# Two squared-ReLU FFNs: from up and down in turn to all up first, then down as seven Strassen products

## The chip, the core and the metric

The kernel runs on one core of a Trainium2 chip. It has a matmul engine (TensorE, PE in the profile, with its weight loads as PEld), three engines for elementwise work (VectorE, DVE; ScalarE, ACT; GpSimd, POOL), a sync engine (SP) that issues all DMAs of this kernel in its own order, and 16 DMA engines. The metric is the time of one execution on the device in microseconds, as the median of several runs.

## The reference

Two transformer blocks, one after the other, on 1024 tokens of width 1024, all in float32. The first mixes tokens by a gated delta rule and by latent attention, the second by a short convolution and stick-breaking attention. Each ends with the FFN that this change is about:

```python
D_MODEL, SEQ, D_FF = 1024, 1024, 4096
# block 1
h = rms_norm(x, ffn_pre_norm[l])
f = jnp.square(jax.nn.relu(h @ w_up[l])) @ w_down[l]
x = x + rms_norm(f, ffn_post_norm[l])
# block 2
h2 = modulate(rms_norm_2(x, g_pre_mlp[l]), sh2, sc2)      # mod = c @ w_ada[l] + b_ada[l]
ff = jnp.square(jax.nn.relu(h2 @ w_mlp_in[l])) @ w_mlp_out[l]
x = x + gt2[:, None, :] * rms_norm_2(ff, g_post_mlp[l])
```

## The kernel before, in words

Every float32 product is made of three matmuls: each operand is split into a part `hi` in a rounded 32-bit format and a rest `lo`, and `mm3` (L166 to L171) adds hi hi, hi lo and lo hi in PSUM. `load_w` (L182) loads 1 MB of weights into one buffer (`w_raw`, a single one), casts it on ACT to `w_hi` (L200, in two halves) and subtracts on DVE to `w_lo` (L206); of `w_hi` and `w_lo` there are two each. `split` (L173) does the same for other tiles.

The two FFNs run in `ffn` (L962). The 4096 columns of `w_up` are cut into 16 chunks of 256; the 1024 tokens into two halves of 512. `up(c, half)` makes two tiles of 128 features x 512 tokens, 24 matmuls each, in feature order, so that a tile is the stationary operand of the down projection as it stands. ACT applies ReLU and the square (L975, L976), DVE squares again and subtracts for the `lo` part (L977, L978). `down(c, half)` multiplies chunk c by 256 rows of `w_down`: for each of 4 token tiles and 2 halves of the 1024 output columns 6 matmuls in PSUM, and DVE adds the result to `y` in SBUF (L1019; `y` holds all 1024 tokens). So up and down alternate, and nothing of f leaves SBUF. In the first FFN `side(c)` works off the modulation of block 2 beside it: `modulation_acc` (L1050) loads four pieces of `w_ada`, one buffer `ada_raw`, and adds their rows on DVE; `modulation_sum` has a matmul, and `modulation_columns` makes `amod` and `mod` out of them.

An `epilogue` (L925) finishes a tile of 128 tokens: it squares `y` on ACT, multiplies by the gain (`yg`, POOL or DVE), takes the inverse root on DVE (`rsqrt`, L212, small operations), adds the residual (`xt`) and stores it. `norm_to_hT` (L267) then normalizes, transposes on PE (L281) and splits into `h_hi` and `h_lo`, the next layer's input. The out projection ahead of each FFN does the first four token tiles, then the last four, so the second half of h comes later than the first; the order of the first steps in `ffn` (L1023 to L1030) is made for that.

A scheduler puts the instructions of each engine in a fixed order, by priority (the order in the program, `tc.high_priority` ahead of it) and by its own estimate of times. A tile's buffers are handed out in turn; a new tile waits until the old one's users are done. Each engine, SP too, then works strictly in its order.

Of the kernel before, what the change touches and what calls it, by code (L numbers as in the profile page):

```python
# [8 lines left out]
F32 = mybir.dt.float32  # L9
# [16 lines left out]
# columns of the constant array  # L26
# [11 lines left out]
}  # L38
FSLOTS = 3

# rows of the vector table (columns once transposed)
# [4 lines left out]
def constants():  # L46
# [6 lines left out]
    # from the first to the second 32 of each 64  # L53
# [11 lines left out]
def tile_two_blocks(ctx: ExitStack, tc: tile.TileContext, I, out):  # L65
# [9 lines left out]
    class Ring:  # L75
        # a pool for each buffer: a new pool waits for all that its memory was used for, so the smaller the sooner
# [40 lines left out]
    def interleave(*streams, bg=None):  # L117
        # streams of (generator, total cost): emit so that all of them advance evenly;
        # bg: one more that is left where it stands when the others have ended
# [14 lines left out]
    # ------------------------------------------------------------------ scratch in DRAM  # L134
# [21 lines left out]
    mix_dr = scratch("mix", (D, S))  # L156

    # ------------------------------------------------------------------ helpers
# [53 lines left out]
    def rsqrt(ssq, scale, eps, n=1, name="rs", pool=None):  # L212
        # v^-1/2, v = scale ssq + eps: a first guess from the bits of v (within 3.5%), three Newton steps
# [27 lines left out]
    # ------------------------------------------------------------------ constants  # L241
# [11 lines left out]
    def columns(st):  # L253
# [50 lines left out]
    # ------------------------------------------------------------------ block 1: projections  # L304
# [7 lines left out]
    def rotary(p1, cs, fr, posi):  # L312
# [20 lines left out]
        # token-major: cos cos -sin sin  # L333
# [6 lines left out]
    def rotary_T(p1, cs, csC, csS):  # L340
        # feature-major, four heads: (cos cos) x 4 and (-sin sin) x 4
# [10 lines left out]
    def block1_low_rank(h, px, p1, wkp, cqT, ckT, cs):  # L352
# [26 lines left out]
            # both halves of k by themselves; the second one comes where the next weights lie later  # L379
# [67 lines left out]
            # decay and write strength: la = -exp(a_log) softplus(ga + dt_bias), beta = sigmoid(gb)  # L447
# [17 lines left out]
    def mla_up(pa, cqT, ckT, csC, csS):  # L465
# [28 lines left out]
        # columns regrouped: nope of all heads, rope of all heads, rope with its halves swapped  # L494
# [32 lines left out]
    # silu(gate) * out_norm  # L527
# [16 lines left out]
    # q, k, v: causal convolution, silu  # L544
# [32 lines left out]
    # ------------------------------------------------------------------ block 1: gated delta rule  # L577
    # chunks of 128 tokens, four heads side by side
# [26 lines left out]
    def blocks_of(t, c, b):  # L605
        # block b of chunk c in each head: [row, head, column]
# [4 lines left out]
    # all that needs neither q nor v: normalized k, decays, A = strictly lower part of beta k k^T decay  # L611
    def gdn_keys(kp):
# [3 lines left out]
        # exp of: cumulative decay, decay to the chunk's end, whole chunk's decay  # L616
# [6 lines left out]
        def head(hd, k):  # L623
            # four chunks of a head side by side
# [778 lines left out]
```

## Time and profile before

| | us |
|---|---|
| median of 3 runs | 2857.09 (2855.22 to 2857.35) |
| span of the profiled execution, first to last instruction | 2851.6 |
| PE busy in that span | 2787.7 |
| first FFN, first up matmul to the last down matmul, about | 653.7 to 1385 |
| second FFN, the same, about | 2138 to 2838 |

The profile is of one execution. It gives for each engine the busy time and the time of every instruction; a wait is put down to what released it. Matmuls are pipelined: the length shown of one is not the step from one to the next.

### The profile page before, as it was taken

The page shows a single profiled execution, that of the slowest core. Times are in us where ns is not written, and L with a number is a line of the kernel's source. Part 1 is how long each engine was busy: PE and PEld are TensorE (multiplying, and loading weights), DVE is VectorE, ACT ScalarE, POOL GpSimd, SP SyncE. Part 2 cuts the span into 40 slices and gives each one's busy share as a digit, 9 for nine tenths or more (in the row PEclk, how much of TensorE's full clock was granted, in tenths as well). Part 3 has the DMA queues.
Part 4 walks back from the last instruction along what each step waited for, and adds up shares of the span by engine and source line. Part 5 has one row for each costly group of instructions (what it writes and reads, how often), then busy time and mean ns, then how long its engine had stood idle before and what let it go on. Part 6 is the DMA issues. An engine that isn't in the chain of part 4 may idle for free. (4 is left out here: it accounts for less than half of the span.)

```text
span 2851.6 us, 39066 instructions
## 1 busy us (share of the span) xinstructions
PE 2787.7 (98%) x14568; PEld 2362.7 (83%) x14568; DVE 1837.8 (64%) x3805; ACT 1079.8 (38%) x2083; POOL 363.6 (13%) x472
## 2 busy tenths in 40 slices
PE   7999999999999999999999999999999999999998
PEld 7788889898787787878898888887898888888886
DVE  7668699868677666557833258776477454444457
ACT  5544666555311212124621146563266221121122
POOL 1242353211000000001200022112212000000000
PEclk9999999999999999999999999999999999999999
DMA  4386486355433233113441545445754211111124
GB/s 129 93 289 197 153 236 166 123 166 184 146 96 111 89 96 94 55 60 128 168 152 63 173 135 154 128 128 164 249 178 155 74 59 45 45 60 36 54 85 144
DMA packets 306885, 360.84 MB, mean 127 GB/s; under 512 B 29844, under 2 KB 240891, under 8 KB 306695
## 3 DMA queue, kind: packets, MB, share of 16 engines
q1 hardware_dynamic: 306694, 358.35, 39.6%
q8 instruction: 115, 1.88, 0.3%
q14 instruction: 76, 0.61, 0.1%
HBM read 278.80 MB, written 79.48 MB: 126 GB/s over the span
## 5 line engine op out<-in xcount | busy, mean ns | idle before, releaser
L170 PE MATMUL mm<-h_hi,w_hi 128*128 128x512 f32 x1760 | 690.5, 392 | 0.0
L170 PE MATMUL mm<-h_lo,w_hi 128*128 128x512 f32 x1760 | 689.1, 392 | 0.0
L170 PE MATMUL mm<-h_hi,w_lo 128*128 128x512 f32 x1760 | 688.1, 391 | 0.0
L170 PE MATMUL mm<-w_hi,f 128*128 128x512 f32 x2048 | 649.0, 393 | 1.8 <-ACT w_hi L200 1.1
L200 ACT CAST w_hi<-w_raw 128x1024 fp32r<-128x1024 f32 (+1 forms) x282 | 282.3, 1047 | 616.4 <-PE mm L170 470.0
L206 DVE TENSOR_TENSOR w_lo<-w_raw,w_hi 128x1024 fp32r<-128x1024 f32 (+1 forms) x282 | 347.0, 1250 | 228.6 <-ACT w_hi L200 226.0
L170 PEld LDWEIGHTS mm<-w_hi,f 128*128 128x128 f32 x2048 | 384.3, 188 | 90.4 <-ACT w_hi L200 1.6
L1019 DVE TENSOR_TENSOR y<-y,mm 128x512 f32<-128x512 f32 x464 | 315.8, 685 | 160.5 <-PE mm L170 158.3
L170 PE MATMUL mm<-w_lo,f 128*128 128x512 f32 x1024 | 401.8, 393 | 0.0
L170 PEld LDWEIGHTS mm<-h_hi,w_hi 128*128 128x128 f32 x1760 | 330.7, 188 | 76.0 <-DVE y L1019 7.8
L170 PEld LDWEIGHTS mm<-h_hi,w_lo 128*128 128x128 f32 x1760 | 330.8, 188 | 66.4
L170 PEld LDWEIGHTS mm<-h_lo,w_hi 128*128 128x128 f32 x1760 | 330.9, 188 | 65.8 <-issue 0.2
L975 ACT ACTIVATE f_r<-mm 128x512 f32<-128x512 f32 x128 | 76.2, 595 | 543.1 <-PE mm L170 542.9
L170 PEld LDWEIGHTS mm<-w_lo,f 128*128 128x128 f32 x1024 | 192.2, 188 | 42.8
L977 DVE TENSOR_TENSOR f_r<-f_r 128x512 f32<-128x512 f32 x128 | 88.0, 688 | 164.5 <-ACT f L976 164.4
L170 PE MATMUL mm<-w_hi,mixT 128*128 128x256 f32 x1024 | 187.6, 285 | 5.3 <-DVE m_sg L1243 2.9
L170 PEld LDWEIGHTS mm<-w_hi,mixT 128*128 128x128 f32 x1024 | 160.5, 192 | 7.0 <-ACT w_hi L200 3.3
L170 PE MATMUL mm<-w_lo,mixT 128*128 128x256 f32 x512 | 145.3, 285 | 1.7 <-DVE w_lo L206 1.7
L1060 DVE SCALAR_TENSOR_TENSOR ada_acc<-ada_raw,vec,ada_acc 128x128 f32<-128x128 f32 x336 | 119.3, 355 | 8.8
L1203 DVE TENSOR_TENSOR_SCAN s_r<-s_r,zero 128x128 f32<-128x128 f32 (+3 forms) x96 | 97.7, 1020 | 38.3 <-POOL s_r L1201 36.9
L933 POOL TENSOR_TENSOR yg<-y,gpost 128x1024 f32<-128x1024 f32 x10 | 26.7, 2670 | 746.2 <-issue 658.3
L276 POOL TENSOR_SCALAR y<-xt,nrsy 128x1024 f32<-128x1024 f32 x16 | 24.6, 1538 | 728.3 <-DVE ersy L223 719.7
(348 smaller groups left out, 4118.3 us busy)
## 6 DMA issues: line engine op xcount, KB each, us to landing
w_raw<-in_w_in SPq DMA_DIRECT2D x32, 1024.0 KB
ada_raw<-in_w_ada SPq DMA_DIRECT2D x48, 512.0 KB
w_raw<-in_w_up SPq DMA_DIRECT2D x21, 1024.0 KB
w_raw<-in_w_down SPq DMA_DIRECT2D x21, 1024.0 KB
w_raw<-in_w_mlp_in SPq DMA_DIRECT2D x21, 1024.0 KB
w_raw<-in_w_mlp_out SPq DMA_DIRECT2D x21, 1024.0 KB
w_raw<-in_w_out SPq DMA_DIRECT2D x16, 1024.0 KB
xres<-xt SPq DMA_DIRECT2D x24, 512.0 KB
```

Of the source, the lines that this page charges most:

```text
L170: PE.matmul(ps, l, r, start=first and n == 0, stop=final and n == last)
L200: ins = ACT.copy(wh[:, step * i:step * i + step], raw[:, step * i:step * i + step])
L206: DVE.tensor_tensor(out=wl[:, c], in0=raw[:, c], in1=r32(wh[:, c]), op=ALU.subtract)
L276: POOL.tensor_scalar(xn, xt, rs, 1.0, ALU.mult, ALU.mult)
L933: eng.tensor_tensor(out=yg, in0=y, in1=gbc, op=ALU.mult)
L975: ACT.activation(r, ps, AF.Relu)
L977: DVE.tensor_tensor(out=r, in0=r, in1=r, op=ALU.mult)
L1019: DVE.tensor_tensor(out=y[:, t, ns], in0=y[:, t, ns], in1=ps, op=ALU.add)
L1060: DVE.scalar_tensor_tensor(out=a, in0=raw[:, k, :], scalar=col(R_C + k), in1=a, op0=ALU.mult, op1=ALU.add)
L1203: DVE.tensor_tensor_scan(out=rest[:, cs_][:, ::-1], data0=rest[:, cs_][:, ::-1], data1=zero.to_broadcast([P, c1 - c0]), initial=rest[:, c1 ...
```

## The change

Each FFN runs in two phases.

*Up.* All 16 chunks of `up` run first (`ffn_up`). A tile f of 128 features x 512 tokens is ReLU and square, unsplit, in float32 (two passes on ACT, in place). Call f11, f12 the tiles of the first token half with even and odd feature blocks, f21, f22 those of the second. For each chunk, f11, f22, and the five sums f11 + f12, f21 - f11, f11 + f22, f21 + f22, f12 - f22 are written to DRAM (`fs_dr`, seven arrays of 4 MB); DVE makes three of the sums, POOL two. The first three chunks of the first token half run ahead of those of the second half, whose order is 2, 1, 0.

*Down.* `ffn_down` makes the seven Strassen products of 512 tokens x 2048 features x 512 columns, in the order 2, 4, 0, 3, 6, 1, 5. Each is summed over its features in four PSUM banks, 8 steps of 2 blocks of 128 features (called chunks from here on). For a step SP loads 512 KB of the left operand (two buffers `dfr`, split into three buffers `df0`, `df1` each) and one or two blocks of 512 KB of the down weights, into `dwr` and `w_raw` in turn; where there are two, POOL adds or subtracts them in place, then the result is split into half of a `w_hi` and `w_lo`. When a product is complete, ACT writes or DVE adds it to one or two quarters of `y`. The first four token tiles are complete after product 6, the last four after product 5.

`y` and the epilogue's buffers now lie where the tiles of `ffn_up` were. The second FFN's epilogue has two `xt` buffers where it had three. Comments are also removed all over the file.

```diff
@@ TAGS @@
+    "fp": "f00*4 f01*4 f10*2 f11*2 fs4 fs5 fs0 fs1 fs6 ada_acc*2 ada_raw f_r",
+    "dp": "dfr*2 df0*3 df1*3 dwr",
-FSLOTS = 3
@@ scratch @@
+    fs_dr = [scratch(f"fs{i}", (P, 16 * 512)) for i in range(7)]
@@ ffn @@
                 after(4 * half + tt)
         return res
-    def ffn(h, w_up, w_dn, y, fp, after, first, side=lambda c: None, last=None):
+    def ffn_up(h, w_up, fp, first, side=lambda c: None):
         NC = w_up.shape[1] // 256
...
+        fs, uw = {}, dict(enumerate(first))
         def up(c, half):
...
             if c not in uw:
                 uw[c] = w_cols(w_up, 256 * c, 256)
-            f = fs[c, half] = [fp.tile([P, 2, 512], F32R, name=f"f{i}", bufs=FSLOTS) for i in range(2)]
             for j in range(2):
                 ps = mm_tile()
...
-                ACT.activation(r, ps, AF.Relu)
-                ACT.activation(f[0][:, j], r, AF.Square)
-                DVE.tensor_tensor(out=r, in0=r, in1=r, op=ALU.mult)
-                DVE.tensor_tensor(out=f[1][:, j], in0=r, in1=r32(f[0][:, j]), op=ALU.subtract)
...
-        def down_last(a, b, half):
...
-        def down(c, half):
...
+                feat_major(ps, j * P, halves[half], h, uw[c])
+                f = fs[c, half, j] = fp.tile([P, 512], F32, name=f"f{half}{j}")
+                ACT.activation(f, ps, AF.Relu)
+                ACT.activation(f, f, AF.Square)
+                if half == 0 or j == 1:
+                    if half != j:
+                        continue
+                    left(c, 2 if half == 0 else 3, f)
+        def left(c, i, t):
+            SP.dma_start(fs_dr[i][:, 512 * c:512 * c + 512], t)
+        def sums(c):
+            f11, f12, f21, f22 = (fs.pop((c, half, j)) for half in range(2) for j in range(2))
+            for i, x, z, op, eng in ((4, f11, f12, ALU.add, POOL), (5, f21, f11, ALU.subtract, DVE),
+                                     (0, f11, f22, ALU.add, POOL), (1, f21, f22, ALU.add, DVE),
+                                     (6, f12, f22, ALU.subtract, DVE)):
+                t = fp.tile([P, 512], F32, name=f"fs{i}")
+                eng.tensor_tensor(out=t, in0=x, in1=z, op=op)
+                left(c, i, t)
         with tc.high_priority(offset=100):
             up(0, 0), up(1, 0)
-        down(0, 0), up(2, 0), down(1, 0)
...
-        up(0, 1), up(1, 1), side(0), down(0, 1), up(2, 1), side(1), down(1, 1)
-        for c in range(3, NC - 2):
-            side(c - 1)
-            up(c, 0), down(c - 1, 0), up(c, 1), down(c - 1, 1)
...
+        up(2, 0)
+        del uw[0]
+        for c in (2, 1, 0):
+            up(c, 1)
+            sums(c)
+            side(2 - c)
+        for c in range(3, NC):
+            up(c, 0), up(c, 1)
+            sums(c)
+            side(c)
+    def ffn_down(w_dn, y, dp, after, last=None):
+        wb = w_dn.rearrange("(s j p) n -> j p s n", j=2, p=P)
+        CH = 2
+        raws = [0]
+        def left(i, c):
+            raw = dp.tile([P, CH * 512], F32, name="dfr")
+            SP.dma_start(raw, fs_dr[i][:, 512 * CH * c:512 * CH * (c + 1)])
+            t = [dp.tile([P, CH * 512], F32R, name=f"df{n}") for n in range(2)]
+            split(t[0], t[1], raw)
+            return [v.rearrange("p (k n) -> p k n", k=CH) for v in t]
+        def right(blocks, sub, c, dst):
+            raws[0] += 1
+            if raws[0] % 2:
+                raw = dp.tile([P, 2 * CH * 512], F32, name="dwr")
+            else:
+                raw = wp.tile([P, 2112], F32, name="w_raw", tag="w_raw", bufs=1)[:, :2 * CH * 512]
+            for n, (j, d) in enumerate(blocks):
+                SP.dma_start(raw[:, n * CH * 512:(n + 1) * CH * 512].rearrange("p (k n) -> p k n", k=CH),
+                             wb[j][:, CH * c:CH * (c + 1), 512 * d:512 * d + 512])
+            a, b = raw[:, :CH * 512], raw[:, CH * 512:]
+            if len(blocks) == 2:
+                POOL.tensor_tensor(out=a, in0=a, in1=b, op=ALU.subtract if sub else ALU.add)
+            split(dst[0], dst[1], a)
+        def product(i, blocks, sub, done):
+            acc = [mm_tile() for _ in range(4)]
+            n = 16 // CH
+            for c in range(n):
+                f = left(i, c)
+                if c % 2 == 0:
+                    w = [wp.tile([P, 2112], F32R, name=nm, tag=nm) for nm in ("w_hi", "w_lo")]
+                o = (c % 2) * CH * 512
+                wc = [t[:, o:o + CH * 512] for t in w]
+                right(blocks, sub, c, wc)
+                wc = [t.rearrange("p (k n) -> p k n", k=CH) for t in wc]
+                for tt in range(4):
+                    tok = slice(tt * P, tt * P + P)
+                    mm3(acc[tt], [(f[0][:, k, tok], f[1][:, k, tok], wc[0][:, k], wc[1][:, k]) for k in range(CH)],
+                        first=c == 0, final=c == n - 1)
+                    if c == n - 1:
+                        done(tt, acc[tt])
+        def to(a, d, tt):
+            return y[:, 4 * a + tt, 512 * d:512 * d + 512]
+        def put(a, d, sign=1):
+            def fn(tt, p):
+                if sign == 1:
+                    ACT.copy(to(a, d, tt), p)
+                else:
+                    ACT.activation(to(a, d, tt), p, AF.Copy, scale=-1.0)
+            return fn
+        def add(a, d, op=ALU.add):
+            return lambda tt, p: DVE.tensor_tensor(out=to(a, d, tt), in0=to(a, d, tt), in1=p, op=op)
+        def all_of(*fns):
+            def fn(tt, p):
+                for g in fns:
+                    g(tt, p)
+            return fn
+        product(2, ((0, 1), (1, 1)), True, all_of(put(0, 1), put(1, 1)))
+        product(4, ((1, 1),), False, all_of(add(0, 1), put(0, 0, -1)))
+        product(0, ((0, 0), (1, 1)), False, all_of(add(0, 0), add(1, 1)))
+        product(3, ((1, 0), (0, 0)), True, all_of(add(0, 0), put(1, 0)))
+        product(6, ((1, 0), (1, 1)), False, all_of(add(0, 0), lambda tt, p: after(tt)))
+        product(1, ((0, 0),), False, all_of(add(1, 0), add(1, 1, ALU.subtract)))
         if last is None:
-            return down_last(a, b, 1)
-        down(a, 1)
-        res = [last(0)]
-        down(b, 1)
-        res.append(last(1))
+            return product(5, ((0, 0), (0, 1)), False, all_of(add(1, 1), lambda tt, p: after(4 + tt)))
+        product(5, ((0, 0), (0, 1)), False, add(1, 1))
+        res = [last(0), last(1)]
         for t in range(4, 8):
             after(t)
         return res
...
@@ program, first FFN @@
-                with sbuf("ep", 1, tags="gpost xt*2 junk yg hmod*2") as ep, sbuf("fp", 2, side="right") as fp:
-                    gf = ep.tile([P, D], F32, name="gpost")
-                    bcast_row(gf, I["ffn_post_norm"][0], D)
-
+            with sbuf("dp", 1, tags=TAGS["dp"]) as dp:
+                with sbuf("fp", 1, side="right", tags=TAGS["fp"]) as fp:
                     pend = {}
 
                     def side(c):
                         if c == 12:
                             modulation_columns(fp)
 
-                    first = ffn(h, I["w_up"][0], I["w_down"][0], y, fp, lambda t: epilogue(
+                    ffn_up(h, I["w_up"][0], fp, first, side)
+                with sbuf("yf", 1, side="right") as yp, sbuf("ep", 1, side="right", tags="gpost xt*2 junk yg hmod*2") as ep:
+                    y = yp.tile([P, NT, D], F32, name="y")
+                    gf = ep.tile([P, D], F32, name="gpost")
+                    bcast_row(gf, I["ffn_post_norm"][0], D)
+                    first = ffn_down(I["w_down"][0], y, dp, lambda t: epilogue(
                         t, y[:, t, :], gf, ep, x_dr[0], x_dr[1],
                         lambda t, xt, xn, junk: norm_to_hT(t, xt, xn, junk, h[0], h[1], gain=amod[:, 0:8], bias=mod[:, 0:8], tmp_pool=ep)),
-                        first, side, lambda i: w_cols(w_in2, (1024, 512)[i], 256))
+                        lambda i: w_cols(w_in2, (1024, 512)[i], 256))
             with sbuf("pb", 2, side="right") as pb:
                 block2_conv_qkv(h, w_in2, pb, first)
@@ program, second FFN @@
...
-                ffn(h, I["w_mlp_in_2"][0], I["w_mlp_out_2"][0], y, fp, lambda t: epilogue(
+            with sbuf("dp2", 1, tags=TAGS["dp"]) as dp:
+                with sbuf("fp2", 1, side="right", tags=TAGS["fp"]) as fp:
+                    ffn_up(h, I["w_mlp_in_2"][0], fp, first)
+                with sbuf("yf2", 1, side="right") as yp, sbuf("ep3", 1, side="right", tags="gpost xt*2 junk yg") as ep:
+                    y = yp.tile([P, NT, D], F32, name="y")
+                    gf = ep.tile([P, D], F32, name="gpost")
+                    gt = ep.tile([P, D], F32, name="junk")
+                    gated_gain(gf, gt, 5, I["g_post_mlp_2"][0])
+                    ffn_down(I["w_mlp_out_2"][0], y, dp, lambda t: epilogue(
+                        t, y[:, t, :], gf, ep, x_dr[2], out[0], None, eng=POOL if t > 5 else DVE))
```

## Rows read from the trace of the kernel before

**Rows 1.** The page: the span, and part 1 (engine, busy us, share, instructions).
```profile
span 2851.6 us, 39066 instructions
...
PE 2787.7 (98%) x14568; PEld 2362.7 (83%) x14568; DVE 1837.8 (64%) x3805; ACT 1079.8 (38%) x2083; POOL 363.6 (13%) x472
```
**Rows 2.** Timeline of PE from 1499.7 us: start, length, what.
```profile
1499.68 0.39 PE L170 MATMUL mm<-h_lo,w_hi 128*128 128x512 f32 x1
1499.91 0.39 PE L170 MATMUL mm<-h_hi,w_lo 128*128 128x512 f32 x1
```
**Rows 3.** The chain that ended last, in order of time: start, us, what.
```profile
2176.43 660.08 PE mm L170 x2912
```
**Rows 4.** Page, part 5: down's matmuls, and DVE's squaring of f: busy us, mean ns.
```profile
L170 PE MATMUL mm<-w_hi,f 128*128 128x512 f32 x2048 | 649.0, 393 | 1.8 <-ACT w_hi L200 1.1
...
L170 PE MATMUL mm<-w_lo,f 128*128 128x512 f32 x1024 | 401.8, 393 | 0.0
...
L977 DVE TENSOR_TENSOR f_r<-f_r 128x512 f32<-128x512 f32 x128 | 88.0, 688 | 164.5 <-ACT f L976 164.4
```
**Rows 5.** Busy windows, second FFN: PE, PEld, DVE, ACT, POOL, clock, DMA share, GB/s.
```profile
2500.00:2760.00 260.00, 260.00 (x1149) 215.44 (x1148) 127.56 (x172) 56.84 (x76) 0.00 (x0) 1.00 0.17 57
```
**Rows 6.** The same view: a stretch of much DMA in the first block.
```profile
142.00:160.00 18.00, 17.46 (x121) 15.42 (x120) 14.01 (x34) 7.85 (x20) 8.38 (x14) 1.00 0.96 329
```
**Rows 7.** Timelines of SP: modulation loads, a 1 MB load, one behind another.
```profile
869.75 24.69 SPq L1056 DMA_DIRECT2D ada_raw<-in_w_ada  x4
...
2052.32 0.38 SPq L195 DMA_DIRECT2D w_raw<-in_w_out  x1
...
2808.41 0.32 SPq L928 DMA_DIRECT2D xt<-xres  x1
2809.18 0.38 SPq L195 DMA_DIRECT2D w_raw<-in_w_mlp_out  x1
```
**Rows 8.** Lines 206 and 933, each by itself: ns shortest/median/longest.
```profile
L206 DVE TENSOR_TENSOR w_lo<-w_raw,w_hi x282: 1027/1220/3434, 11.1 to 2819.5; 128x1024 fp32r<-128x1024 f32 x139, 128x848 fp32r<-128x848 f32 x2
...
L933 POOL TENSOR_TENSOR yg<-y,gpost x10: 2338/2414/3265, 596.3 to 2843.8; 128x1024 f32<-128x1024 f32 x10
```
**Rows 9.** Timelines of ACT: first ReLUs of both FFNs, casts that waited for loads.
```profile
659.14 0.60 ACT L975 ACTIVATE f_r<-mm 128x512 f32<-128x512 f32 x1 [2.97 <-PE mm L170]
...
681.96 2.00 ACT L200 CAST w_hi<-w_raw 128x1024 fp32r<-128x1024 f32 x2 [6.99 <-DMA w_raw<-in_w_up]
...
2057.38 2.00 ACT L200 CAST w_hi<-w_raw 128x1024 fp32r<-128x1024 f32 x2 [5.78 <-DMA w_raw<-in_w_out]
...
2143.44 0.60 ACT L975 ACTIVATE f_r<-mm 128x512 f32<-128x512 f32 x1 [3.20 <-PE mm L170]
...
2817.25 1.05 ACT L200 CAST w_hi<-w_raw 128x1024 fp32r<-128x1024 f32 x1 [5.29 <-DMA w_raw<-in_w_mlp_out]
```
**Rows 10.** Timelines of DVE: the last h_lo of both FFNs, an operation at the end.
```profile
703.28 0.68 DVE L176 TENSOR_TENSOR h_lo<-tr,h_hi 128x512 fp32r<-128x512 f32 x1
...
2179.94 1.70 DVE L291 TENSOR_TENSOR h_lo<-hmod,h_hi 128x512 fp32r<-128x512 f32 x2 [0.51 <-POOL h_hi L290]
...
2839.19 1.93 DVE L219 SCALAR_TENSOR_TENSOR ersb<-ersy,ersg 128x1 f32<-128x1 f32 x1
```
**Rows 11.** Timelines of POOL: a gain ahead of the second FFN, an epilogue at the end.
```profile
2171.33 2.40 POOL L1088 TENSOR_TENSOR gpost<-gpost,junk 128x1024 f32<-128x1024 f32 x1 [7.05 <-issue]
...
2838.76 2.35 POOL L933 TENSOR_TENSOR yg<-y,gpost 128x1024 f32<-128x1024 f32 x1 [658.27 <-issue]
```
**Rows 12.** Busy windows as in rows 5, around a pause of PE.
```profile
2030.00:2040.00 10.00, 5.85 (x26) 4.87 (x25) 5.79 (x7) 3.65 (x5) 2.13 (x1) 0.80 0.74 246
2040.00:2045.00 5.00, 5.00 (x34) 5.00 (x33) 1.85 (x4) 0.00 (x0) 1.28 (x1) 0.71 0.98 311
```
**Rows 13.** Timelines of PE: that pause (idle before, releaser), and the last matmul.
```profile
2035.65 0.35 PE L170 MATMUL mm<-w_hi,mixT 128*128 128x256 f32 x1 [2.86 <-DVE m_sg L1243]
...
2837.47 0.39 PE L170 MATMUL mm<-w_hi,f 128*128 128x512 f32 x1
```

More of the change, by code (lines that the diff above doesn't have):

```diff
@@ L985, in down_last @@
-        def down_last(a, b, half):
-            wf = [(w_down(c), fs.pop((c, half))) for c in (a, b)]
-            p = {}
-            def part(i, g):
-                (w, f), tok, ns = wf[i], slice(P * (g // 2), P * (g // 2) + P), slice(512 * (g % 2), 512 * (g % 2) + 512)
-                if i == 0:
-                    p[g] = mm_tile()
-                mm3(p[g], [(f[0][:, j, tok], f[1][:, j, tok], w[0][:, j, ns], w[1][:, j, ns]) for j in range(2)],
-                    first=i == 0, final=i == 1)
-            for g in range(4):
-                part(0, g)
-            for g in range(8):
-                part(1, g)
-                t, ns = 4 * half + g // 2, slice(512 * (g % 2), 512 * (g % 2) + 512)
-                DVE.tensor_tensor(out=y[:, t, ns], in0=y[:, t, ns], in1=p.pop(g), op=ALU.add)
-                if g + 4 < 8:
-                    part(0, g + 4)
-                if g % 2:
-                    after(t)
@@ L1008, in down @@
-        def down(c, half):
-            w, f = w_down(c), fs.pop((c, half))
-            for tt in range(4):
-                t, tok = 4 * half + tt, slice(tt * P, (tt + 1) * P)
-                for n in range(2):
-                    ns = slice(512 * n, 512 * n + 512)
-                    ps = mm_tile()
-                    mm3(ps, [(f[0][:, j, tok], f[1][:, j, tok], w[0][:, j, ns], w[1][:, j, ns]) for j in range(2)])
-                    if c == 0:
-                        ACT.copy(y[:, t, ns], ps)
-                    else:
-                        DVE.tensor_tensor(out=y[:, t, ns], in0=y[:, t, ns], in1=ps, op=ALU.add)
+                feat_major(ps, j * P, halves[half], h, uw[c])
@@ L1360, in tile_two_blocks @@
     with late:
-        with sbuf("hT2", 1) as hp, sbuf("yp2", 1) as yp, sbuf("ep2", 1, tags="gpost xt*3 junk yg hmod*2") as ep:
+        with sbuf("hT2", 1) as hp:
             h = new_hT(hp)
-            y = yp.tile([P, NT, D], F32, name="y")
-            gb = ep.tile([P, D], F32, name="gpost")
-            gt = ep.tile([P, D], F32, name="junk")
-            gated_gain(gb, gt, 2, I["g_post_mix_2"][0])
-            first = out_projection(I["w_out_2"][0], mrg_dr, y, mxp2, lambda t: epilogue(
-                t, y[:, t, :], gb, ep, x_dr[1], x_dr[2],
-                lambda t, xt, xn, junk: norm_to_hT(t, xt, xn, junk, h[0], h[1], gain=amod[:, 8:16], bias=mod[:, 24:32], tmp_pool=ep)),
-                lambda: [w_cols(I["w_mlp_in_2"][0], 256 * c, 256) for c in range(2)])
-            mx2.close()
-            with sbuf("fp2", 2) as fp:
-                gf = ep.tile([P, D], F32, name="gpost")
-                gt = ep.tile([P, D], F32, name="junk")
-                gated_gain(gf, gt, 5, I["g_post_mlp_2"][0])
-                ffn(h, I["w_mlp_in_2"][0], I["w_mlp_out_2"][0], y, fp, lambda t: epilogue(
-                    t, y[:, t, :], gf, ep, x_dr[2], out[0], None, eng=POOL if t > 5 else DVE), first)
@@ new lines, in tile_two_blocks @@
+            with sbuf("yp2", 1) as yp, sbuf("ep2", 1, tags="gpost xt*3 junk yg hmod*2") as ep:
+                y = yp.tile([P, NT, D], F32, name="y")
+                gb = ep.tile([P, D], F32, name="gpost")
+                gt = ep.tile([P, D], F32, name="junk")
+                gated_gain(gb, gt, 2, I["g_post_mix_2"][0])
+                first = out_projection(I["w_out_2"][0], mrg_dr, y, mxp2, lambda t: epilogue(
+                    t, y[:, t, :], gb, ep, x_dr[1], x_dr[2],
+                    lambda t, xt, xn, junk: norm_to_hT(t, xt, xn, junk, h[0], h[1], gain=amod[:, 8:16], bias=mod[:, 24:32], tmp_pool=ep)),
+                    lambda: [w_cols(I["w_mlp_in_2"][0], 256 * c, 256) for c in range(2)])
+                mx2.close()
```

18 lines of the change are left out of this document (1 added, 17 removed).

## Prediction

> **What bounds the kernel now.** I read the first part of the page, then the matmuls in order of time, then the windows of the second FFN. TensorE (PE) is busy 98% of a span of 2851.6 us, and its granted clock is 1.00 of 2.4 GHz in the long windows [rows 1, 5]. But a busy matmul is not a price: each 128x512 matmul is shown as 0.39 us long, while the next one starts 0.23 us later [rows 2]. The chain of waits ends in one unbroken stretch of 2912 matmuls in 660.08 us [rows 3], so one costs 660.08 / 2912 = 0.2267 us. There nothing but PE counts: in a 260 us window of it DVE is busy 127.56, ACT 56.84, POOL 0, and the DMA engines 17% of the time [rows 5]. So in the FFNs work taken from PE is time gained, as long as the other engines and the DMAs keep their slack. The change spends much of just that slack.
>
> **What is removed.** The down projections are 2048 + 1024 matmuls [rows 4]: per FFN 16 chunks x 2 row blocks x 8 token tiles x 2 column halves x 3 = 1536. Seven products of 8 chunks x 4 tiles x 2 blocks x 3 make 1344. It saves 192 per FFN, 384 in all, x 0.2267 = **87.0 us**. (By the length shown it would be 150, which the starts refute.) The up projections keep their 1536 matmuls (348 us) per FFN. The additions into y after every chunk also go; they were hidden.
>
> **The up phase.** A column chunk is 96 matmuls, 21.8 us. ACT still makes two passes per tile, and the weight casts. DVE's eight operations of 0.69 us [rows 4] become three sums of that size, and POOL gets two of at most half the 2.34 to 3.27 us that it takes for twice the size [rows 8]. SP issues seven writes of 0.26 MB and one weight load of 1.05 MB: 2.9 MB in 21.8 us, 132 GB/s, against 329 GB/s that the DMA engines moved at a share of 0.96 [rows 6]. All hidden, with three exceptions:
> - *The second half of the tokens.* Before, five steps of 48 matmuls (54 us) needed only the first half; now three (32.6 us, some 36 with the last tiles' transposes). The first ReLU of an FFN ends its first 24 matmuls, so up began 5.4 us earlier: 653.7 and 2138.0 [rows 9]. The last h_lo ended at 704.0 and 2181.6 [rows 10], 50 and 44 us later. Unchanged that is a wait of 14 and 8 us. But in the first FFN ACT, and DVE behind it, stood 6.99 us for a third weight load [rows 9], which is now not behind a load of the down weights; in the second POOL made a gain of the FFN's end (2.40 us, [rows 11]) ahead of the last tile, which the change emits later; and DVE loses the eight operations per chunk. I take 5 + 2 = 7 us, of 0 to 22. Queued behind this wait on PE is all of up. A pause that long can cost clock: after a pause of 2.86 us PE's granted clock was 0.80 over 10 us and 0.71 over the next 5 [rows 12], 6.9 us at the lower level of 1.2 GHz, 3.5 us lost; for two pauses 0 to 7, of which I take 0, because the pauses are short.
> - *Weights of chunk 0, loaded again.* The order is chunks 2, 1, 0 and there are two buffers, so its cast waits for the last matmul of chunk 1: 1.05 (ACT, [rows 9]) + 1.22 (DVE, [rows 8]), 2.5 us per FFN with hops, 5 in all, of 0 to 9.
> - *Modulation (first FFN only).* Four loads, one chunk's share, were issued within 24.69 us [rows 7], where 43.5 us passed per chunk; now 21.8 pass. It can run late by tens of us, but PE needs it only for a row of sums and amod only after five products. 2 us, of 0 to 10.
>
> **Between the phases** the first left operand (f11, written throughout) needs a load and a split; all but the last pieces lie in DRAM already, and its last write is due some 16 us before up ends. 2 us per FFN, 4 in all, of 0 to 10.
>
> **The down phase: can it be fed?** A chunk is 24 matmuls, 5.44 us. It needs 0.52 MB of left operand and 0.52 or 1.05 MB of weights. In five of seven products there are two blocks: 1.57 MB in 5.44 us, 289 GB/s, 88% of the 329 above. ACT casts twice (2.1 us), DVE subtracts twice (2.44), POOL adds once (2.41 median) [rows 8, 9]. No engine is over 5.44 alone, so the bound is the cycle of a raw buffer. There are two, so each must turn round in two chunks, 10.88 us:
> - load: 1 MB was usable 5.06 us after its issue with nothing ahead of it (2052.32 to 2057.38) and 8.07 us behind another load (issued at 2808.41; 2809.18 to 2817.25) [rows 7, 9]. Two halves of it, issued one after the other, mostly between the left loads: 5.8.
> - POOL 2.41, ACT 1.05, DVE 1.22, and 0.8 for SP, semaphores and ACT's left casts.
> - waits of POOL and DVE for each other. A subtraction reads two SBUF tiles and the add two: near the end a 128x1 DVE operation took 1.93 us, up to the end of POOL's 2.35 us multiplication, where 128x512 elements take 0.69 [rows 4, 10, 11]. So I let them run one after the other: 2.44 + 2.41 = 4.85 of each 5.44 us. 1.2 us a cycle.
>
> Sum 12.5 us, of 10.5 to 15. The Trainium skill ("SBUF — State Buffer", "SBUF: two separate sides") calls the port pair of these two engines an exclusive lock, which speaks against adds on POOL here. The trace agrees (1.93 us); if they ran side by side, the cycle would be 11.3 and the next term 0.
>
> The weights lie split up to two pairs of chunks ahead, and a one-block product refills that, so a run of two-block products begins with some 8 us in hand. Each pair loses 12.5 - 10.88 = 1.6 us. Products 0, 3, 6 run in a row, 12 pairs: 12 x 1.6 - 8 = 11.4 us. Products 2 and 5 stand alone: 4 x 1.6 is under 8. So 23 us for both FFNs; 0 at a cycle up to 11.5, and at 15 us (4.1 a pair) 41 + 8 + 8 = 57 per FFN, 115 in all. What is late is the split weights, and PE stands at a chunk's first matmul. SP is in order: behind a load that waits for a buffer stand the left loads and, in products 1 and 5, the epilogue's loads and stores.
>
> **The ends.** In the first FFN the last four tiles of y complete within one chunk, about 4 us nearer to the end than the tile that came first before; block 2 has 44 us of first-half work: 1 us, of 0 to 4. The last matmul started at 2837.5, 14 us before the end [rows 13]; the last four tiles now come 1.4 us apart and queue for one `yg` and two `xt` buffers: 2 us, of 0 to 6.
>
> **Sum.** -87.0 + 7 + 5 + 2 + 4 + 23 + 1 + 2 = -43. The profiled span is 2851.6 us; the median of the runs, 2857.1, lies 5.5 above, what stands around the span, and I let that stand. Forecast: span 2808.6, **time 2814 us**. With every cost at its low end it is 2770. With all at the high end (22 + 7 + 9 + 10 + 10 + 115 + 4 + 6 = 183 against 87) it is 2953, but that needs all of them at once.
>
> **Rivals.**
> - *The cover holds.* If the cycle is 11.5 us or less, the feeding term is 0 and the time is 2814 - 23 = 2791 (2775 to 2797). For: no engine is over 90% busy. Against: load latency under load, and the lock. 0.25.
> - *The feeding becomes the bound, and it is slower.* The other costs are 21 us, so feeding must cost 66, 33 per FFN: 20 x (cycle - 10.88) - 24 = 33, a cycle of 13.7 us; from there on it is slower. A load of 7 us instead of 5.8 is enough (1 MB took 8.07 behind another). At 14.5 us it costs 97 and gives 2888. For: a share of 88% leaves queues at the DMA engines. Against: two buffers in opposite phase meet little. 0.13, range 2850 to 2910.
> - *Start of up.* The second half arrives as late as before and PE loses clock: 22 + 7 instead of 7, 2836. It goes with the forecast's range.
> - *The change doesn't do what it says:* reads of the scratch wait for the whole of it. Only product 2 reads what was just written, and one wait of 5 to 8 us per FFN gives about 2826; not a case of its own.
>
> **How the numbers follow.** The forecast with its range 2797 to 2850 has 0.62, the cover 0.25, the slower rival 0.13. The range 2778 to 2862 leaves out a little of the cover's low end and most of the slower rival. A measurement of this kernel tells 0.2% (5.7 us) from no change: under 2851.4 is faster, over 2862.8 slower. 0.84, 0.05 and 0.11.
>
> **What would show it.** In the profile after: 384 fewer 128x512 matmuls with w and f at the same step of 0.227 us; a pause of PE of some us about 36 us after each up phase begins; steps between chunks in products 0, 3 and 6 of about 6 us and of 5.44 in 1 and 4; POOL's adds at 2.4 us or over, with DVE's subtractions stretched beside them. It is wrong if matmuls in the down phase step more slowly, if left loads from the scratch land much later than weights, or if PE's clock falls in the down phase.

## The result, and the profile after

The median after is **2927.3 us** (2916.9 to 2931.6 in four runs), beside 2856.7 (2855.2 to 2857.4) before on the same chip: a ratio of 1.0241, 95% interval 1.0227 to 1.0255. The change makes the kernel 70.6 us slower; 2814 was forecast, with a range up to 2862. The profiled execution took 2916.9 us with a span of 2915.1, the fastest of the four, so the stages below, with 2.0 us ahead of the first ReLU, add up to 63.5 us of the 70.6. The kernel before, run again beside each group of experiments, had medians of 2856.7 to 2858.7; differences of two or three us between runs tell nothing.

The page of the kernel after, where [rows 1] stood:
```profile
span 2915.1 us, 39462 instructions
...
PE 2745.2 (94%) x14184; PEld 2317.3 (79%) x14184; DVE 1712.3 (59%) x3361; ACT 1210.6 (42%) x2207; POOL 664.1 (23%) x616
```
The 384 matmuls are gone (14568 to 14184), yet PE is busy 94% and not 98%: some 170 us of the span without a matmul, where there were 64. The next table says where. It is read from the timelines: the first and the last ReLU of each up phase, the last addition into y of each FFN, the last copy into c_u (the second block's first stage), each by its start, and the end of the span.

| stage, us | before | after | no modulation, before | no modulation, after | best version (last chunks tile by tile) |
|---|---|---|---|---|---|
| first FFN, first ReLU to last addition into y | 725.9 | 803.7 | 709.9 | 672.1 | 693.5 |
| of this up, first to last ReLU | | 485.4 | | 348.0 | 366.6 |
| to the last c_u copy | 148.9 | 161.4 | 148.9 | 159.5 | 152.2 |
| to the second FFN's first ReLU | 609.5 | 609.1 | 608.7 | 609.2 | 612.0 |
| second FFN, first ReLU to last addition into y | 695.2 | 658.9 | 695.8 | 657.5 | 659.7 |
| from there to the end | 13.0 | 21.0 | 13.2 | 21.2 | 14.8 |

The second FFN gained 36 us. The first one lost 78, and the place is its up phase: 485.4 us, where the same 1536 matmuls in the second FFN take 348.1 (1536 x 0.2266). Windows of the kernel after: the first up phase, its worst part, and the second FFN's stretch of [rows 5] (the columns are those of [rows 5]):
```profile
655.00:1150.00 495.00, 418.87 (x1651) 322.31 (x1651) 250.55 (x542) 135.00 (x203) 61.11 (x39) 0.90 0.51 161
...
900.00:1000.00 100.00, 71.46 (x247) 51.12 (x246) 47.86 (x105) 19.68 (x29) 9.04 (x6) 0.81 0.43 135
...
2500.00:2760.00 260.00, 257.31 (x1133) 212.04 (x1132) 111.84 (x91) 93.37 (x111) 79.83 (x34) 1.00 0.64 219
```
In the worst part PE is busy 71 of 100 us at a granted clock of 0.81, while DVE, ACT and POOL are each busy less than half of the time and the DMA engines have 43%. Nothing is full, so something waits in a circle. What PE waited for between 655 and 1150 us (us in total, times, longest):
```profile
PE mm L1106 <- DVE ada_acc L1100: 35.8, 10, 7.6
PE mm L172 <- DVE w_lo L208: 19.7, 7, 6.0
PE mm L172 <- ACT w_hi L202: 7.3, 8, 0.9
PE mm L172 <- ACT f L977: 7.0, 1, 7.0
PE mm L172 <- ACT f_r L1107: 5.5, 8, 0.9
```
L1106 is the modulation's row sum. The view of its tile ada_raw in the same kernel (operation, count: ns shortest/median/longest, first and last start; then the idle time in front of it):
```profile
L1096 SPq DMA_DIRECT2D ada_raw<-in_w_ada x48: 368/384/910, 682.0 to 1113.3; - x48
...
  DMA ada_raw<-in_w_ada: 192.4, 45
```
48 loads go through one buffer. From first to last issue pass 431.3 us over 47 steps, **9.2 us** a piece: SP waits until DVE has summed the piece, issues, the data land, DVE sums. Four pieces are 36.7 us, and a chunk gives them 21.8. DVE stood 192.4 us in order before 45 of these loads.

The pauses cost clock as well. PE around one of them, in order of time (start, length; idle before and its releaser):
```profile
907.43 1.86 PE L1106 MATMUL mm<-ada_acc,cst 128*1 128x512 f32 x2 [4.42 <-DVE ada_acc L1100]
...
910.55 0.63 PE L172 MATMUL mm<-h_lo,w_hi 128*128 128x512 f32 x1
910.97 0.63 PE L172 MATMUL mm<-h_hi,w_lo 128*128 128x512 f32 x1
```
After 4.42 us of waiting the matmuls step by 0.42 us instead of 0.23, the lower of the clock's two levels (the granted clock is 0.50 from 909.5 to 911.5). So the 137 us that the up phase lost are about 76 us of waits (the list above with 0.7 of smaller ones), 24 row-sum matmuls x 0.59 = 14, and a rest of 47 that is for the most part clock. A mean of 0.90 over 495 us makes 49.5 us, but that counts the waits too: by the trace's record of the clock some 36 us were lost while PE was busy. The 11 us between 36 and 47 are not explained.

### The profile page after: what moved, and what is told of

The parts are those of the page before. It is cut to its first block, busy times and chain, and to the rows that moved or that the text cites. A ratio compares the mean times of both kernels' runs of the same rounds, so it can differ in the third digit from the quotient of the medians.

```text
span 2915.1 us, 39462 instructions
## 1 busy us (share of the span) xinstructions
PE 2745.2 (94%) x14184; PEld 2317.3 (79%) x14184; DVE 1712.3 (59%) x3361; ACT 1210.6 (42%) x2207; POOL 664.1 (23%) x616
## 5 line engine op out<-in xcount | busy, mean ns | idle before, releaser
L172 PE MATMUL mm<-w_hi,df 128*128 128x512 f32 x1792 | 556.6, 391 | 7.9 <-ACT y L1061 5.9
L172 PEld LDWEIGHTS mm<-w_hi,df 128*128 128x128 f32 x1792 | 337.0, 188 | 80.5 <-ACT y L1061 6.7
L172 PE MATMUL mm<-w_lo,df 128*128 128x512 f32 x896 | 350.9, 392 | 3.4 <-DVE w_lo L178 3.0
L208 DVE TENSOR_TENSOR w_lo<-w_raw,w_hi 128x1024 fp32r<-128x1024 f32 (+1 forms) x182 | 228.0, 1279 | 168.9 <-ACT w_hi L202 168.4
L202 ACT CAST w_hi<-w_raw 128x1024 fp32r<-128x1024 f32 (+1 forms) x182 | 182.2, 1047 | 309.3 <-PE mm L172 218.7
L178 DVE TENSOR_TENSOR df<-dfr,df 128x1024 fp32r<-128x1024 f32 x112 | 156.3, 1408 | 104.4 <-ACT df L177 95.6
L172 PEld LDWEIGHTS mm<-w_lo,df 128*128 128x128 f32 x896 | 168.9, 188 | 42.0 <-DVE w_lo L178 7.2
L1034 POOL TENSOR_TENSOR dwr<-dwr 128x1024 f32<-128x1024 f32 x40 | 103.1, 2579 | 328.1 <-DMA dwr<-in_w_mlp_out 177.8
L993 DVE TENSOR_TENSOR fs<-f,f 128x512 f32<-128x512 f32 x96 | 84.6, 901 | 145.7 <-ACT f L978 145.7
L177 ACT CAST df<-dfr 128x1024 fp32r<-128x1024 f32 x112 | 115.8, 1050 | 122.8 <-PE mm L172 77.1
L178 DVE TENSOR_TENSOR w_lo<-dwr,w_hi 128x1024 fp32r<-128x1024 f32 x56 | 95.6, 1707 | 103.6 <-ACT w_hi L177 103.2
```

Source lines behind the costliest of these rows:

```text
L172: PE.matmul(ps, l, r, start=first and n == 0, stop=final and n == last)
L177: ACT.copy(hi, src)
L178: DVE.tensor_tensor(out=lo, in0=src, in1=r32(hi), op=ALU.subtract)
L202: ins = ACT.copy(wh[:, step * i:step * i + step], raw[:, step * i:step * i + step])
L208: DVE.tensor_tensor(out=wl[:, c], in0=raw[:, c], in1=r32(wh[:, c]), op=ALU.subtract)
L993: eng.tensor_tensor(out=t, in0=x, in1=z, op=op)
```

## Experiments

Theory: the modulation's chain through one buffer, hidden at the old pace of 43.5 us a chunk, is slower than the new pace and holds PE. Rival: the scratch traffic and the feeding of the down phase cost it.

**Two buffers.**
```diff
-            raw = pool.tile([P, KT, P], F32, name="ada_raw", bufs=1)
+            raw = dp.tile([P, KT * P], F32, name="dfr").rearrange("p (k n) -> p k n", k=KT)
```


> Changed against the kernel after: the pieces of w_ada go to the two buffers dfr that the down phase has and the up phase does not need, instead of to one ada_raw. Theory (the chain load, sum, load through one buffer, 9.05 us a piece and 36 us a chunk, sets the pace of the first up phase, which PE could run in 21.8 us a chunk): the first up phase shrinks from 490 us to 375 to 400, and the time falls by 90 to 115 us to 2810 to 2835. Rival 1 (the loss is in the writes and reads of the scratch and in the down phase): no change, 2915 to 2930. Rival 2 (the row sums on PE and the sums on DVE cost by their own length, not by the wait for the buffer): at most half of the loss goes, 2860 to 2890.

Measured: 2833.8 us (2830.7 to 2837.4), 93 less than after; the up phase takes 396.2 us. Both lie in the theory's ranges. What PE still waits for, 655 to 1100 us:
```profile
PE mm L1106 <- DVE ada_acc L1100: 8.8, 4, 3.9
PE mm L172 <- DVE w_lo L208: 8.7, 5, 3.9
PE tr L1118 <- DVE ada_acc L1115: 4.0, 1, 4.0
PE mm L1106 <- ACT f L977: 2.9, 1, 2.9
```

**No modulation, in the kernel after and in the kernel before.** The same edit in both:
```diff
-                        if c < 12:
-                            pend[c] = modulation_acc(c, fp)
-                        if c - 1 in pend:
-                            modulation_sum(c - 1, pend.pop(c - 1), fp)
-                        if c == 12:
-                            modulation_columns(fp)
+                        if c == 0:
+                            DVE.memset(mod, 0.0)
+                            DVE.memset(amod, 1.0)
...
+                                    SP.dma_start(mod_dr[r:r + 1, 512 * k:512 * k + 512], z[0:1, :])
```

> Changed against the kernel after: the modulation is left out altogether (its loads, its sums on DVE and its row sums on PE); mod is set to 0 and amod to 1. Theory: the first up phase takes what the second one takes, 353 us instead of 490, of which some 20 us are the row sums themselves; time 2775 to 2800. Rival 1 (scratch and down phase): only the 20 us of row sums go, 2895 to 2910.

Measured: 2781.7 us (2780.6 to 2782.3). The up phase takes 348.0 us, as in the second FFN, and its window of 655 to 1150 us reads
```profile
655.00:1150.00 495.00, 494.16 (x2198) 409.37 (x2197) 193.84 (x217) 182.32 (x249) 98.67 (x55) 1.00 0.54 180
```
with PE full at the full clock. All of the 145.7 us goes with the modulation, and none of the up phase's loss stays for the scratch writes.

> Changed against the kernel before: the modulation is left out altogether (loads, sums on DVE, row sums on PE); mod is set to 0 and amod to 1. Theory (at the pace of before, 43.5 us a chunk, the chain of 36 us a chunk was hidden, and the modulation cost PE only its row sums, 24 matmuls of 0.59 us and their hops, some 15 to 20 us): 2837 to 2843. Then the change without modulation is worth 2781.7 less this, about -58 us. Rival (the modulation already cost PE waits before): under 2830.

Measured: 2842.2 us (2841.8 to 2844.0), ratio to before 0.995 (0.9935 to 0.9965). So the modulation cost 15.1 us before and 145.7 after, 130.6 more, and the rest of the change is worth 2781.7 - 2842.2 = **-60.6 us**.

**Loads issued by POOL, still one buffer.**
```diff
-            SP.dma_start(raw, I["w_ada_2"][0][:, c0:c0 + P].rearrange("(k p) n -> p k n", p=P))
+            POOL.dma_start(raw, I["w_ada_2"][0][:, c0:c0 + P].rearrange("(k p) n -> p k n", p=P))
```


> Changed against the kernel after: the loads of w_ada are issued by POOL instead of SP, still into one buffer; so the loads of w_up and the writes of the scratch no longer stand behind a load that waits for the buffer. Theory (the cycle of the one buffer, with DVE and PE in order behind it): the pace stays at 33 to 36 us a chunk, 2890 to 2930. Rival (what costs is SP's order: loads of w_up and writes behind the waiting loads): most of the loss goes, 2820 to 2850.

Measured: 2970.8 us (2966.5 to 2982.4), beyond what either expected: 43 more than after. Taking the waiting loads out of SP's order doesn't shorten the cycle of the buffer. The tile's view of this run:
```profile
L1096 POOL DMA_DIRECT2D ada_raw<-in_w_ada x48: 882/884/1106, 683.1 to 1164.8; - x48
```
and POOL in order of time:
```profile
900.33 0.88 POOL L1096 DMA_DIRECT2D ada_raw<-in_w_ada  x1 [7.02 <-DVE ada_acc L1100]
...
906.38 2.78 POOL L993 TENSOR_TENSOR fs<-f,f 128x512 f32<-128x512 f32 x2 [5.17 <-issue]
```
An issue takes 0.88 us instead of 0.38, a piece (1164.8 - 683.1) / 47 = 10.2 us, and POOL's sums of quarters now stand behind the wait for the buffer. So POOL's order took the place of SP's, and this run doesn't tell what SP's order alone costs. The Trainium skill ("Trainium Kernel Development and Optimization", Key Constraints) says that issuing from several engines only saves the sequencer's issue time; this trace agrees in that a piece came no sooner (10.2 us against 9.2), and an issue took longer on POOL's queue than on SP's.

**No row sums, but the loads and DVE's sums.** Zeros and ones stand in for what is left out.
```diff
                         if c < 12:
                             pend[c] = modulation_acc(c, fp)
-                        if c - 1 in pend:
-                            modulation_sum(c - 1, pend.pop(c - 1), fp)
-                        if c == 12:
-                            modulation_columns(fp)
...
```

> Changed against the kernel after: the loads of w_ada through one buffer and their sums on DVE stay, but the row sums on PE, their copies and stores and the columns are left out; mod is set to 0 and amod to 1. It tells which queue hands the delay on to PE. Theory (DVE, in order: the subtractions that make w_lo and the sums of quarters stand behind a sum that waits for its load): the pace stays near 36 us a chunk and only the row sums themselves go, 2880 to 2915. Rival (PE, in order: matmuls stand behind a row sum that waits for DVE): most of the loss goes, 2790 to 2850.

Measured: 2848.3 us (2843.0 to 2855.4). My theory for this run fell: 79 us went, and only 14 are the row sums' own. The PE waits between 655 and 1150 us:
```profile
PE mm L172 <- DVE w_lo L208: 23.4, 8, 3.9
PE mm L172 <- DVE w_lo L178: 18.7, 3, 13.8
```
The chain is as slow as before (first piece summed at 688.8, last one begun at 1130.7), but the up phase ends at 1065 and PE leaves the chain behind, until the down phase's first weights stand behind it on DVE (13.8 us). So more than one queue handed the delay on. PE, in order, tied itself to the chain by the row sum of each chunk: 79 - 14 = 65 us, with the row sum's copy on ACT and its store on SP, which go with it here. DVE, in order, held w_lo back, and this run stays 66.6 us above the one without modulation. How these 66.6 divide between DVE's order and SP's (the loads of w_up behind waiting loads) was not tried. But SP has a part in it, as the wait of 13.8 us shows (timelines of SP, DVE and PE):
```profile
1060.30 8.35 SPq L985 DMA_DIRECT2D fs<-fs  x2
...
1066.55 1.75 DVE L993 TENSOR_TENSOR fs<-f,f 128x512 f32<-128x512 f32 x1
...
1069.08 0.38 SPq L1096 DMA_DIRECT2D ada_raw<-in_w_ada  x1
...
1073.51 0.29 DVE L1098 TENSOR_SCALAR ada_acc<-ada_raw,vec 128x128 f32<-128x128 f32 x1 [4.94 <-DMA ada_raw<-in_w_ada]
...
1074.10 1.22 DVE L178 TENSOR_TENSOR w_lo<-dwr,w_hi 128x1024 fp32r<-128x1024 f32 x1
...
1075.37 0.80 PE L172 MATMUL mm<-w_lo,df 128*128 128x512 f32 x1 [13.78 <-DVE w_lo L178]
```
The w_hi of this w_lo was ready at 1060.1, but the subtraction stood in DVE's order behind two pieces, and the load of the second stood in SP's order behind the write of a sum that DVE had yet to make, itself behind the first piece. So the two orders held each other. The Trainium skill ("PSUM — Partial Sum Buffer", Engine vs sequencer instructions) calls VectorE's queue strict FIFO and has matmuls start in program order; the trace agrees: the w_lo waits above, and the 65 us that went with the row sums.

**Two pieces a chunk, one buffer.** A third of the pieces is left out.
```diff
+                    PACE = 2
...
-                        if c < 12:
-                            pend[c] = modulation_acc(c, fp)
-                        if c - 1 in pend:
-                            modulation_sum(c - 1, pend.pop(c - 1), fp)
+                        for i in [i for i in pend if 4 * i + 4 <= done[0]]:
+                            modulation_sum(i, pend.pop(i), fp)
+                        while done[0] < min(32, PACE * (c + 1)):
...
+                            modulation_piece(i, q, pend[i], fp)
+                            done[0] += 1
```

> Changed against the kernel after: still one buffer ada_raw, but two pieces of w_ada per chunk in all 16 chunks instead of four in the first 12; the last 16 of the 48 pieces and their four row sums are left out (those columns stay zero); a row sum comes one chunk after its last piece, and the columns are made after the third product of the down phase. Theory (throughput: two cycles of the one buffer are 18.1 us and fit into a chunk of 21.8 us, so one buffer costs nothing by itself): the run without modulation plus 16 row-sum matmuls of 0.59 us and a wait at the last one, 2790 to 2805. Rival (each load for which DVE and SP stand in order costs PE time, whatever the pace): 32 pieces cost two thirds of what 48 did, 2840 or more.

Measured: 2800.7 us (2798.3 to 2802.6), in the theory's range and 19 over the run without modulation; 9.4 of it are 16 row sums. The longest of PE's waits between 655 and 1130 us:
```profile
PE mm L172 <- DVE w_lo L208: 2.8, 2, 2.4
```
and the view of the tile ada_raw, the loads and the idle time in front of the sums:
```profile
L1094 SPq DMA_DIRECT2D ada_raw<-in_w_ada x32: 377/384/427, 685.3 to 981.5; - x32
...
  DMA ada_raw<-in_w_ada: 118.3, 32
```
This is the run that settles it: one buffer, 9.6 us a piece, DVE idle 118 us waiting for the 32 loads, and PE loses 2.8. That there are fewer pieces doesn't explain it: at a price per piece two thirds of the loss would have stayed. The columns come later here too, but PE's waits in the kernel after have none for them. A wait on an engine with slack cost next to nothing here; what cost 130 us was a cycle longer than the time it was given.

**Spread pieces, two buffers.** All 48 pieces; row sums and columns late as above.
```diff
+        raw = dp.tile([P, KT * P], F32, name="dfr").rearrange("p (k n) -> p k n", k=KT)
...
+                    PACE = 3.3
...
+                        while done[0] < min(48, PACE * (c + 1)):
```

> Changed against the kernel after: as in the run with two buffers, but the 48 pieces of w_ada are spread over 14.5 chunks (3.3 a chunk instead of 4 in each of the first 12), each row sum comes one chunk after its last piece, and the columns are made after the third product of the down phase. Theory (what is left of the loss with two buffers, 52 us above the run without modulation, is still PE and DVE meeting pieces that are not there): only the row sums stay, 2797 to 2812. Rival (DVE's own work, 14 us of sums a chunk beside the casts, is what is left): 2825 to 2835 as with two buffers.

Measured: 2812.2 us (2806.6 to 2813.7), ratio to before 0.9837 (0.9821 to 0.9854): at the upper end of the theory's range. Up takes 370.4 us, 14 of the 22 over 348 being row sums.

**Free buffers at both ends.**
```diff
+        xt = xp.tile([P, D], F32, name="dfr") if xp else ep.tile([P, D], F32, name="xt")
...
-                        t, y[:, t, :], gf, ep, x_dr[2], out[0], None, eng=POOL if t > 5 else DVE))
+                        t, y[:, t, :], gf, ep, x_dr[2], out[0], None, eng=POOL if t > 5 else DVE, xp=dp if t > 5 else None))
```


> Changed against the run with spread pieces: in both FFNs the residual rows of the last two token tiles are loaded into the buffers dfr, which are free by then, instead of the two buffers xt, where a load waits for the store of an earlier tile. Theory (21 us from the last addition into y to the end, 8 more than before, are load after store in two buffers): 7 to 9 us less at the end and 0 to 4 less between the first FFN and the second block, 2786 to 2803. Rival (the end is set by DVE and POOL, which share the last four tiles): within 3 us of the run with spread pieces.

Measured: 2802.3 us (2800.7 to 2806.7). The time lies in the theory's range, but its place does not bear the theory out. Of the 7.0 us between the two spans (2812.0 and 2805.0) the end gave 2.6 (21.2 to 18.6), the transition 0.7 (160.9 to 160.2), and 3.7 is the balance of stages before and between, the up phase above all, where the edit changes nothing. What held the end in the kernel after, and what holds it here:
```profile
2899.72 0.32 SPq L930 DMA_DIRECT2D xt<-xres  x1
...
2900.18 0.34 SPq L938 DMA_DIRECT2D out<-xt  x1
...
2904.29 1.28 DVE L937 SCALAR_TENSOR_TENSOR xt<-yg,ersy,xt 128x1024 f32<-128x1024 f32 x1 [0.93 <-DMA xt<-xres]
2905.41 0.32 SPq L930 DMA_DIRECT2D xt<-xres  x1
...
2909.92 1.28 DVE L937 SCALAR_TENSOR_TENSOR xt<-yg,ersy,xt 128x1024 f32<-128x1024 f32 x1 [4.34 <-DMA xt<-xres]
```
```profile
2792.57 2.34 POOL L935 TENSOR_TENSOR yg<-y,gpost 128x1024 f32<-128x1024 f32 x1 [18.34 <-DVE xt L937]
...
2795.63 1.28 DVE L937 SCALAR_TENSOR_TENSOR dfr<-yg,ersy,dfr 128x1024 f32<-128x1024 f32 x1
...
2796.99 2.34 POOL L935 TENSOR_TENSOR yg<-y,gpost 128x1024 f32<-128x1024 f32 x1 [2.08 <-DVE dfr L937]
```
The wait for the load of xt is gone; in its place each POOL product waits until DVE has read the one buffer yg. So the rival was nearer on the place (DVE and POOL in turn, through one buffer), and wrong on the time, which fell by 9.9 us.

**Last chunks tile by tile.** In product 5 the last three chunks, in product 6 the last two, are run tile after tile.
```diff
+                if n - g <= c < n - 1:
+                    continue
                 for tt in range(4):
...
-                        first=c == 0, final=c == n - 1)
+                    for b, x, wc in held:
...
+                            first=b == 0, final=b == n - 1)
```


> Changed against the run with spread pieces and free buffers at the ends: the last three chunks of the last product (two of the fifth) run tile by tile, so that the tiles of y are complete 4.1 (2.7) us apart instead of 1.4. Theory (the end, 18.6 us after the last addition into y, and the first transposes of the second block wait because four epilogues meet): the end is 12 to 15 us, as before the change, and the transition 2 to 6 us shorter; 2790 to 2800. Rival (the longer hold of left operands and weights makes PE wait at the last chunks by as much): 2800 to 2806.

Measured: **2798.3 us** (2792.4 to 2802.1), ratio to before 0.9792 (0.9777 to 0.9807), 129 us under the kernel after. The end is 14.8 us, as expected, and the transition 152.2, 8 us shorter where 2 to 6 were expected. It is the best version here that computes the whole, though its runs overlap those of the one before (2800.7 to 2806.7).

**The second FFN alone.**
```diff
-                    ffn_up(h, I["w_up"][0], fp, first, side)
...
+                    first = ffn(h, I["w_up"][0], I["w_down"][0], y, fp, lambda t: epilogue(
...
+                        first, side, lambda i: w_cols(w_in2, (1024, 512)[i], 256))
```

> First FFN as in the kernel before, second FFN as in the kernel after. Theory (the form itself is worth its 43.5 us of matmuls less some 15 per FFN, and the first one loses by the modulation): 28 us faster than before, 2825 to 2833. Rival (the scratch and the feeding cost more than the matmuls save in either FFN): 2857 or slower.

Measured: 2829.7 us (2826.8 to 2834.8), ratio 0.9904 (0.9888 to 0.9921). The form itself gains 27 to 29 us where no modulation runs beside it.

## Why the prediction was wrong, step by step

- **The step that failed: modulation**, 2 us of 0 to 10; it costs 130.6 more than before. The row was there. [Rows 7] show four issues in 24.69 us, and the prediction set this beside 21.8 us without alarm. Four issues are three steps: (24.69 - 0.37) / 3 = 8.1 us each, so a chunk needs 4 x 8.1 = 32.4 us. Over 12 chunks that is 12 x (32.4 - 21.8) = 127 us. That it comes so near to 130.6 is luck in part: with the 9.2 us a piece of the kernel after the same sum gives 12 x (36.7 - 21.8) = 179, more than the 137 that the up phase lost. The last four chunks (87 us) have no pieces, and the last load is issued only 33 us before the last ReLU, so part of the delay ran out beside them. "It can run late by tens of us" treats a rate as a single delay. A chain that is slower than its host gets later with every round, and two acc buffers, a row sum in PE's queue and sums in DVE's queue leave it no room. The prediction named PE's need "only for a row of sums"; 12 of those in order were enough. Clock was weighed for the start of the phase alone; here it cost 36 us or more.
- **Matmul price and count** were right: 348.1 us for 1536 matmuls, 384 fewer. Without the modulation the change gives -60.6 us; the prediction's sum without its modulation term was -87 + 42 = -45. That this is only 16 us off is luck in part, since the terms below miss in both directions: 28 us too much for the FFNs, 16 too little behind them. They are read from the table's two columns without modulation:
- **Second half of the tokens, and chunk 0 loaded again** (7 and 5 us): nothing. The second up phase runs in 348.1 us, and PE waits for nothing in it. The forecast pause some 36 us into up did not come.
- **Between the phases and feeding** (4 + 23): 709.9 - 672.1 = 37.8 and 695.8 - 657.5 = 38.3 us gained of 43.5 each, so 5.7 + 5.2 = 10.9 lost. The cycle was nearly right in size, its price was not. The chain of the kernel after, in the second down phase, is the raw buffer's cycle as it was written down:
```profile
2665.71 7.18 DMA w_raw<-in_w_mlp_out
2673.05 3.05 POOL w_raw L1034
2676.12 1.06 ACT w_hi L177
2677.21 1.24 DVE w_lo L178
2678.46 0.37 SPq L1030
2678.88 5.34 DMA w_raw<-in_w_mlp_out
...
2749.88 7.01 DMA w_raw<-in_w_mlp_out
```
Seven cycles take 2749.88 - 2665.71 = 84.2 us: 12.0 each, not 12.5. They are made up otherwise: the seven loads take 6.4 us on average instead of 5.8, and POOL's adds 2.7 instead of 2.41, while DVE's subtractions stand at 1.24, so POOL's and DVE's waits for each other are some 0.3 us of a cycle and not 1.2. By the prediction's own formula that is 12 x 1.14 - 8 = 5.7 us per FFN. That 5.7 and 5.2 were lost is luck, though. PE's waits between 2584 and 2895 us:
```profile
PE mm L172 <- ACT y L1061: 3.1, 1, 3.1
PE mm L172 <- DVE w_lo L178: 1.9, 2, 1.1
PE mm L172 <- DVE y L1067: 0.8, 1, 0.8
```
Late weights cost 1.9 us (0.4 in the same FFN without modulation), so the weights in hand covered more than the 8 us allowed for them. In products 0, 3 and 6 of this FFN the chunks step by 5.44 us but for four of 24, not by about 6. The largest wait, 3.1 us (2.7 without modulation), is a term that the prediction doesn't have: product 6 begins only when ACT has copied product 3 out of PSUM into y. The rival "feeding becomes the bound" (33 per FFN) is out, and though it had the right side, it had it for the wrong reason. The rival "cover holds" (0) put the cycle too low, at 11.5 or less, but its price was the nearer one.
- **DVE and POOL one after the other** was right as a mechanism. POOL and DVE in the same stretch:
```profile
2659.72 3.20 POOL L1034 TENSOR_TENSOR w_raw<-w_raw 128x1024 f32<-128x1024 f32 x1
...
2660.71 3.30 DVE L178 TENSOR_TENSOR w_lo<-dwr,w_hi 128x1024 fp32r<-128x1024 f32 x1
2664.04 1.23 DVE L178 TENSOR_TENSOR w_lo<-w_raw,w_hi 128x1024 fp32r<-128x1024 f32 x1
```
The first subtraction takes 3.30 us instead of 1.23 beside POOL's add, which ends at 2662.92, 1.1 us before the subtraction does. What it is worth in a cycle stands above.
- **First FFN to second block** (1 us, of 0 to 4): 159.5 - 148.9 = 10.6 us. PE had first-half work of the second block, 14 us of it, and then met a transpose that POOL had not fed:
```profile
1474.13 0.39 PE L172 MATMUL mm<-h_hi,w_lo 128*128 128x512 f32 x1
1478.04 1.97 PE L283 MATMUL tr<-cst,y 128*128 128x128 f32 x8 [3.53 <-POOL y L278]
1479.66 0.78 PE L172 MATMUL mm<-h_hi,w_hi 128*128 128x512 f32 x1
```
In PE's order the transposes stood ahead of most of the 44 us that the prediction counted on. Four tiles complete at once instead of one after the other; running the last chunks tile by tile took 8 us of this back (160.2 to 152.2).
- **The end** (2 us, of 0 to 6): 8 us, the two buffers xt that were named, with too small a size: a load of xt, issued only after the store of an earlier tile, is used some 4.5 us later, twice in a row (2899.72 to 2904.29 and 2905.41 to 2909.92, in the lines shown with the free buffers).

## What to carry to other kernels

When a phase is shortened, work out the rate of everything that rides along in it: its cycle times its count per round, against the round's new length, and not its delay. Where the cycle is longer, the difference counts up to once per round; give it a second buffer, spread it over more rounds, and keep its consumers out of the bound engine's queue until they are surely ready. Where the last results of a phase come together, the epilogue's buffers are read as serial.

## What was not expected of the hardware

Loads issued by POOL took 0.88 us of its queue each, against 0.38 on SP, and made a chain of load and sum 1 us longer per piece. A row-sum matmul took 0.59 us at the higher clock and up to 1.06; the pair at 907.43, at a granted clock of 0.50, took 1.86.
